# A written list of 2,418 step numbers in place of a list scheduler for the first phase of a decoder-layer kernel

## The chip, the cores and the metric

The kernel runs on one core of a Trainium2 chip. The metric is the device time of one execution, in microseconds (us); the median of the runs before the change is 1961.02 us.

## The reference

One decoder layer over 1024 tokens of width 1024, in float32. The input is normalised and multiplied by `w_in`. Eight query heads of width 64, in two key groups, then run three attentions whose results are added with learned gates: over compressed keys, over selected blocks (with 16 blocks of 64 keys and `n_sel` 16 every block is taken, so this one is causal attention over all keys), and over a window of 512. A second branch gates 512 channels with a triangular 128x128 product in chunks. Both are normalised and multiplied by `w_out`, and a mixture of 32 experts, four per token, follows.

```
h = rmsnorm(x, norm1_g);  z = h @ w_in
o_attn = nsa_attention(q, kc, vc, k_sel, vs, k_win, vw, gates)
o_gm = spatial_gating(zu, zv, gm_v_norm_g, gm_w_s, gm_b_s)
x = x + concat(rmsnorm(o_attn), rmsnorm(o_gm)) @ w_out
x = x + moe(rmsnorm(x, norm2_g), ...)    # top 4 of 32, clamped SwiGLU
```

## The kernel before

Every float32 product is made of three half-precision products: each operand is split into a high part (a copy on ACT) and a low part (the difference, on DVE), and PE multiplies high by high, high by low and low by high. Most stages therefore hand work round in a ring: PE into PSUM, ACT reads it (high), DVE reads it (low), PE again.

The program has two large phases. The **first phase** runs to the router. Its parts are: the transposes of x (line 418), 72 products of x with `w_in` (lines 468 to 470, nine pieces of columns by eight token tiles; `L438` and `L442` split the weights), the compressed keys, the gating branch (`L670`, `L679`, `L683`), the attention, the product with `w_out` (lines 1337 to 1339, one row tile at a time) and the choice of experts (`L1368` to `L1414`). The attention is cut into 48 units of one group, one query tile and one branch. A unit has scores (`L935`, `L936`, into one of three PSUM banks `s`), distances and row maximum in one DVE pass (`L939`), the exponential on ACT (`L919`), and then for each block of keys four transposes on PE (`L976`, into one of three banks `b`), the high part (`L980`, ACT), the low part (`L984`, DVE) and the product with the values (`L996`, PE). `L959` and `L960` make a unit's weights, `L1009` applies them, and POOL adds the three branches (`L1025`, `L1021`).

The **second phase** computes the experts. Its weights come in pieces of 1 MB through five buffers (`L1773`), are split (`L1780` on ACT, `L1783` on DVE) and multiplied (`L1826` to `L1828`).

The order of each engine's instructions is fixed when the program is built. Each stage is registered as steps: `op(engine, cost, function, due, reads, writes)`. `Plan.run` then keeps, for each engine, the time at which it is free, and takes as the next step the one that can start first; steps that can start within 0.05 us of each other are ordered by `due`. The emitted instructions run on the chip in that order on each engine, and wait for each other by semaphores; the planner's own times go nowhere else. In the first phase each `due` was shifted by a number of a table, `WHEN`, one for each group of steps (`plan.group()` opens the next group). A step that needs another engine's result was taken to get it 0.25 us after that one's end, or 2.25 us where it is a load of SP:

```
lag = lag if lag is not None else 2.25 if eng == "sp" else 0.25
```

The experts have a plan of their own, of the same class, without a table: `plan = Plan(rings)`. Rings such as `psS=(3, 1)` and `psT=(3, 1)` in the first plan are the banks `s` and `b`: a step that takes one waits until the user three turns earlier is done.

Of the kernel before, what the change touches and what calls it, by code (L numbers as in the profile page):

```python
# [21 lines left out]
D = 1024  # L22
# [14 lines left out]
def visits(room):  # L37
# [36 lines left out]
WHEN = [  # L74
# [60 lines left out]
class Plan:  # L135
# [8 lines left out]
    def group(self):  # L144

        self.at += 1
# [110 lines left out]
def layer_kernel(ctx: ExitStack, tc: tile.TileContext, x, norm1_g, w_in, q_norm_g, k_norm_g, cmp_pos,  # L257
# [873 lines left out]
    def biases(due):  # L1131
# [34 lines left out]
        for n in range(2):  # L1166
            op("pe", 0.95, lambda n=n: up(n), due, r=[r], w=[b[n]])
# [879 lines left out]
```

## Time and profile before

| what | value |
|---|---|
| median of 3 runs | 1961.02 us (1959.91 to 1964.04) |
| the profiled execution | 1960.88 us, of which the span of its instructions is 1959.1 us |
| PE busy | 1865.3 us, 95% of the span |
| DVE, ACT, POOL busy | 1653.5, 1468.2, 783.0 us |
| mean granted TensorE clock | 0.985 |

The span runs from the first to the last instruction; 1.8 us of the execution lie outside it. An engine's busy time counts the instructions, not the waits of its queue. PE's matmuls are pipelined and their ends are modelled, so that the next one can start before the row of the last one ends; how much work PE has is therefore better read from the distance between the starts of matmuls that follow each other without a wait. A granted clock of 1.00 is 2.4 GHz, 0.50 is 1.2 GHz.

### The profile page before, as it was taken

The numbers are of one execution on the slowest core, as the hardware profiler recorded it, in microseconds if no ns is written. First come the engines' busy times: TensorE is split into PE (matmuls) and PEld (weight loads), VectorE is DVE, ScalarE is ACT, GpSimd is POOL, SyncE is SP. The second block draws the span as 40 slices with busy tenths as digits, with TensorE's granted clock in tenths as the row PEclk, the third lists the DMA queues.
The fourth block names the chain that finished last, engine by engine and source line by source line (L and its number), as shares of the span: only waits on it lengthen the run. The fifth ranks groups of instructions, "written<-read, shape, count | busy, mean of one in ns | idle before, by whom it ended". The sixth has DMA issues, their size and how long they took to land.

```text
span 1959.1 us, 60049 instructions
## 1 busy us (share of the span) xinstructions
PE 1865.3 (95%) x25170; PEld 1708.0 (87%) x25170; DVE 1653.5 (84%) x2844; ACT 1468.2 (75%) x2310; POOL 783.0 (40%) x667
## 2 busy tenths in 40 slices
PE   7999999898996999999999999999999999999996
PEld 6898777666655898899999999999999999999995
DVE  5577887778777898798998999999999999999893
ACT  6566878757554675777877888788888888888883
POOL 0111112345551454344344443353444535455432
PEclk9999999999996999999999999999999999999998
DMA  4320102221125998899999999999999999999993
GB/s 162 84 60 12 45 12 65 87 71 45 66 76 191 299 342 275 282 328 322 336 332 331 339 350 356 338 354 358 363 352 352 350 359 355 351 356 365 361 348 90
DMA packets 244775, 485.88 MB, mean 248 GB/s; under 512 B 20034, under 2 KB 29394, under 8 KB 244498
## 3 DMA queue, kind: packets, MB, share of 16 engines
q1 hardware_dynamic: 230658, 441.19, 64.2%
q0 software_dynamic: 12800, 40.79, 9.2%
q8 instruction: 199, 3.26, 0.7%
q14 instruction: 78, 0.64, 0.1%
q10 hardware_dynamic: 1040, 0.00, 0.0%
HBM read 450.94 MB, written 31.00 MB: 246 GB/s over the span
## 4 chain that ended last, share of the span: by engine, by line
PE 75%; DVE 9%; DMA 7%; ACT 5%; issue 3%; POOL 1%; SPq 0%; DVEq 0%; POOLq 0%; ACTq 0%
PE g L1826 16%; PE g L1827 16%; PE g L1828 16%; PE s L468 3%; PE s L469 3%; PE s L470 3%; DVE par L939 3%; DMA xw<-in_w_gate_up_dram 2%; PE b L1894 2%; PE b L976 2%; PE o L996 2%; DVE wl L1783 2%; DMA raw<-in_w_gate_up_dram 2%; ACT wh L1780 2%; PE b L1752 1%
## 5 line engine op out<-in xcount | busy, mean ns | idle before, releaser
L1826 PE MATMUL g<-xar,wh 128*128 128x88 f16 (+21 forms) x4096 | 770.8, 229 | 0.5 <-ACT ott L1877 0.5
L1827 PE MATMUL g<-xar,wh 128*128 128x88 f16 (+21 forms) x4096 | 771.0, 229 | 0.0
L1828 PE MATMUL g<-xar,wl 128*128 128x88 f16 (+21 forms) x4096 | 770.5, 229 | 0.1
L1783 DVE SCALAR_TENSOR_TENSOR wl<-xw,wh 128x2048 f16<-128x2048 f32 x308 | 714.4, 2326 | 40.2 <-ACT wh L1780 34.6
L1780 ACT ACTIVATE wh<-xw 128x2048 f16<-128x2048 f32 x308 | 626.4, 2036 | 157.2 <-PE g L1827 86.9
L1827 PEld LDWEIGHTS <-wh 128*128 128x128 f16 x6144 | 600.4, 98 | 15.9 <-issue 4.8
L1826 PEld LDWEIGHTS <-wh 128*128 128x128 f16 x6144 | 600.8, 98 | 10.7
L1828 PEld LDWEIGHTS <-wl 128*128 128x128 f16 x6144 | 600.3, 98 | 11.0 <-DVE wl L1783 0.3
L1854 POOL TENSOR_TENSOR aar<-t,aar 128x136 f16<-128x136 f32 (+21 forms) x256 | 360.1, 1423 | 469.1 <-ACT aar L1852 441.9
L1826 PE MATMUL g<-aar,wh 128*128 128x120 f16 (+21 forms) x2048 | 385.4, 229 | 3.8 <-DVE t L1841 3.8
L1828 PE MATMUL g<-aar,wl 128*128 128x120 f16 (+21 forms) x2048 | 385.4, 229 | 0.0
L1827 PE MATMUL g<-aar,wh 128*128 128x120 f16 (+21 forms) x2048 | 385.4, 229 | 0.0
L1841 DVE TENSOR_SCALAR t<-g,bias 128x120 f32<-128x120 f32 (+20 forms) x512 | 170.8, 364 | 32.5 <-PE g L1828 22.4
L1780 ACT ACTIVATE wh<-raw 128x2048 f16<-128x2048 f32 x76 | 154.8, 2037 | 39.6 <-PE g L1827 21.5
L1904 POOL DMA_INDIRECT out_dram<-orow,ix x51 | 124.8, 2447 | 147.7 <-ACT orow L1897 84.4
L1783 DVE SCALAR_TENSOR_TENSOR wl<-raw,wh 128x2048 f16<-128x2048 f32 x76 | 175.4, 2308 | 8.3 <-ACT wh L1780 7.7
L1722 POOL DMA_INDIRECT xg<-xn_d,ix x51 | 128.0, 2510 | 117.2 <-PE g L1828 47.2
L468 PE MATMUL s<-wh,xw 128*128 128x256 f16 (+1 forms) x576 | 158.2, 275 | 1.2 <-DVE mx L939 1.1
L469 PE MATMUL s<-wl,xw 128*128 128x256 f16 (+1 forms) x576 | 158.1, 275 | 0.0
L470 PE MATMUL s<-wh,xw 128*128 128x256 f16 (+1 forms) x576 | 158.0, 274 | 0.0
L1025 POOL TENSOR_TENSOR ob<-ob 128x512 f32<-128x512 f32 x32 | 40.7, 1270 | 191.9 <-DVE ob L1009 164.9
L1849 DVE SCALAR_TENSOR_TENSOR t<-t 128x136 f32<-128x136 f32 (+21 forms) x256 | 100.4, 402 | 18.1 <-ACT t L1846 15.1
(380 smaller groups left out, 2942.0 us busy)
## 6 DMA issues: line engine op xcount, KB each, us to landing
xw<-in_w_gate_up_dram SPq DMA_DIRECT2D x205, 1024.0 KB
xw<-in_w_down_dram SPq DMA_DIRECT2D x103, 1024.0 KB
raw<-in_w_gate_up_dram SPq DMA_DIRECT2D x51, 1024.0 KB
raw<-in_w_down_dram SPq DMA_DIRECT2D x25, 1024.0 KB
wr<-in_w_in_dram SPq DMA_DIRECT2D x16, 512.0 KB
xs<-in_x_dram SPq DMA_DIRECT2D x8, 512.0 KB
wr<-in_w_out_dram SPq DMA_DIRECT2D x8, 512.0 KB
x<-in_x_dram SPq DMA_DIRECT2D x8, 512.0 KB
```

What stands on the lines that cost most here:

```text
L468: mm(o, xa, wh, start=(k == 0), stop=False)
L469: mm(o, xa, wl, start=False, stop=False)
L470: mm(o, xb, wh, start=False, stop=(k == KD - 1))
L1722: nc.gpsimd.indirect_dma_start(out=xg.t[:w], out_offset=None, in_=xn_d, in_offset=bass.IndirectOffsetOnAxis(ap=ix.t[:w, 0:1], axis=0))
L1780: nc.scalar.activation(ws.v[0], raw_.v, AF.Copy, scale=SW)
L1783: nc.vector.scalar_tensor_tensor(ws.v[1], raw_.v, SW, ws.v[0], op0=ALU.mult, op1=ALU.subtract)
L1826: mm(o, wh, xa, start=(kh == 0 and k == 0), stop=False)
L1827: mm(o, wh, xb, start=False, stop=False)
L1828: mm(o, wl, xa, start=False, stop=(kh == 1 and k == 3))
L1841: nc.vector.tensor_scalar(t.t[:, s, :c], ps[s].t[:, :c], self.bias(2 * h + s), m, op0=ALU.add, op1=o)
L1854: plan.op("pool", 0.9 + c / 440, lambda: nc.gpsimd.tensor_tensor(out=self.a[:, h, 1], in0=t.t[:, 1, :c], in1=self.a[:, h, 0], op=ALU.subtr ...
L1904: self.plan.op("pool", 2.0, lambda: nc.gpsimd.indirect_dma_start(out=out, out_offset=bass.IndirectOffsetOnAxis(ap=ix.t[:w, 0:1], axis=0), ...
```

## The change

The first phase's steps are emitted in the order of a list, `STEPS`: 2,418 numbers, one for each step in the order in which the code registers them. The scheduler's choice is left out where such a list is given. `WHEN`, `group()` and all its calls go. Some planned costs and all planned handover times get other numbers. Where a list is given they decide nothing; the experts' plan has no list, so for it the new default handovers (`HANDOVER`) count: 4.0 us behind a load of SP in place of 2.25, and 0.15 to 0.22 behind the engines in place of 0.25.

```
-WHEN = [
-    1346.1, 299.4, 788.3, -170.5, 1081.8, 114.3, -565.0, 519.3, -380.7, 1232.6, -82.9, 90.6, -610.6, 327.8, 529.5, -374.5, 361.1,
...
+STEPS = [
+    0, 7, 67, 4, 1, 8, 19, 9, 68, 31, 10, 69, 11, 5, 12, 43, 13, 16, 70, 14, 6, 79, 17, 2, 71, 189, 72, 15, 20, 76, 3, 73, 55, 74,
...
+HANDOVER = dict(sp=4.0, pe=0.22, act=0.17, dve=0.15, pool=0.2)
...
-    def op(self, eng, cost, fn, due, r=(), w=(), use=(), lag=None, table=None):
+    def op(self, eng, cost, fn, due, r=(), w=(), use=(), lag=None, table=None, own=0.0):
...
-        due += self.when[self.at] if self.at < len(self.when) else 0
...
-        lag = lag if lag is not None else 2.25 if eng == "sp" else 0.25
+        lag = HANDOVER.get(eng, 0.25) if lag is None else lag
...
-        for _ in range(n):
+        for turn in range(n):
             best = None
-            for eng, cand in avail.items():
+            for eng, cand in () if self.seq else avail.items():
...
+            if self.seq:
+                best = ready(self.seq[turn]), self.seq[turn]
...
-            end[i] = free[eng] = t + cost
+            end[i] = free[eng] = max(t, free[eng]) + cost
...
-                     m=(2, 0), ogt=(1, 0), x1=(2, 0), xn=(1, 0), xt=(1, 0), xp=(1, 0), s2=(2, 0), jo=(1, 1)), WHEN)
+                     m=(2, 0), ogt=(1, 0), x1=(2, 0), xn=(1, 0), xt=(1, 0), xp=(1, 0), s2=(2, 0), jo=(1, 1)), STEPS)
...
-        op("pe", 0.45, run, due, r=[("wsT", g)] + toks, w=[y])
+        op("pe", 0.86, run, due, r=[("wsT", g)] + toks, w=[y])
...
-        op("pe", 2.7, hidden, due + 8, r=[w1] + parts, w=[hp], use=[xc])
+        op("pe", 3.55, hidden, due + 8, r=[w1] + parts, w=[hp], use=[xc])
```

How the instructions move is seen at three places. The new file has other line numbers; its line in the rows below is told where the text needs it.

First, ACT in the attention, at the third of the four places where it makes the gating branch's GELU (`L683`, now 724; `L980` is now 1015, `L1126` 1158, `L679` 720, `L919` 956, `L846` 884). Before:

```order
L980 ACTIVATE ph<-b 128x512 x3
L679 ACTIVATE ubuf<-s 128x256
L683 ACT_TABLE_LOAD
L683 ACTIVATE ubuf<-ubuf 128x1024
L980 ACTIVATE ph<-b 128x512 x2
L1126 ACTIVATE xw<-wr,gms 128x1024
L980 ACTIVATE ph<-b 128x512 x2
L690 ACTIVATE ubuf,sso<-vb 128x256 x4
```

Now:

```order
L1158 ACTIVATE xw<-wr,gms 128x1024
L720 ACTIVATE ubuf<-s 128x256
L724 ACT_TABLE_LOAD
L724 ACTIVATE ubuf<-ubuf 128x1024
L1015 ACTIVATE ph<-b 64x512
L1158 ACTIVATE xw<-wr,gms 128x1024
L884 ACTIVATE q_160<-b,gqh 128x512
L956 ACT_TABLE_LOAD
L956 ACTIVATE par,su<-par,mx 128x896
L1015 ACTIVATE ph<-b 128x512
```

In the old order two high parts of transposed probabilities, then a piece of `w_out`, then two more follow the GELU; in the new one the high parts stand apart. PE's order has to do with it: before, 16 transposes (four blocks of keys) stand in a row there,

```order
L996 LDWEIGHTS ph
L996 MATMUL o<-vv,ph 128x128
L996 LDWEIGHTS pl
L996 MATMUL o<-vv,pl 128x128
L976 MATMUL b<-ident,par 128x128 x16
L996 LDWEIGHTS ph
L996 MATMUL o<-vv,ph 128x128
```

and at the last of these four blocks PE now has, with scores (972 and 973) and a product with the values (1031) around each block's four transposes (1011),

```order
L1031 MATMUL o<-vv,ph 128x128
L1031 LDWEIGHTS pl
L1031 MATMUL o<-vv,pl 128x128
L972 LDWEIGHTS q_160
L972 MATMUL s<-ka_149,q_160 128x256
L973 LDWEIGHTS q_160
L973 MATMUL s<-kb_150,q_160 128x256
L1011 MATMUL b<-ident,par 128x128 x4
L972 LDWEIGHTS q_159
L972 MATMUL s<-ka_149,q_159 128x256
L973 LDWEIGHTS q_159
L973 MATMUL s<-kb_150,q_159 128x256
```

In all of the first phase, transposes of probabilities stood in 81 runs of one block, 21 of two, 7 of three and 1 of four; now there are 98, 16, 6 and 0.

Second, DVE at the first of the router's choices (`L1368` to `L1414`, now 1394 to 1440). Before:

```order
L1009 TENSOR_TENSOR ob<-o,su 128x512
L1368 TENSOR_REDUCE lr<-b 128x32
L1369 SCALAR_TENSOR_TENSOR lg<-lr,brb 128x32
L1411 MAX mx_5614<-lg 128x8
L1412 COPY rep<-mx_5614 128x4
L1413 MATCH_REPLACE lr<-rep,lg 128x32
L1414 TENSOR_TENSOR sel_5618<-lg,lr 128x128
L959 RECIPROCAL su<-su 128x4
L960 TENSOR_TENSOR su<-su,gates 128x4
L984 SCALAR_TENSOR_TENSOR pl<-b,ph 128x512
L1257 SCALAR_TENSOR_TENSOR ml<-b,mh 128x512
```

Now (976 is `L939`, 994 to 996 are `L958` to `L960`):

```order
L1394 TENSOR_REDUCE lr<-b 128x32
L1395 SCALAR_TENSOR_TENSOR lg<-lr,brb 128x32
L1437 MAX mx_5458<-lg 128x8
L1438 COPY rep<-mx_5458 128x4
L1439 MATCH_REPLACE lr<-rep,lg 128x32
L1440 TENSOR_TENSOR sel_5462<-lg,lr 128x128
L976 ISA ptc,mx<-s,dcmp 128x64
L976 ISA mx 128x1
L976 ISA par,mx<-s,dist,mx 128x512
L976 ISA mx 128x1
L994 TENSOR_SCALAR su<-su 128x4
L995 RECIPROCAL su<-su 128x4
```

Before, a low part for PE (`L984`) stood three rows behind the choice; now row maxima and a unit's weights stand there.

Third, DVE at the opening of the second phase, where the list doesn't reach: `xar` and `ixf`, `ix`, `gtt` are the gathered tokens and their indices and gates, `oh` the one-hot rows that pick them (`L1701`). Before:

```order
L1783 SCALAR_TENSOR_TENSOR wl<-xw,wh 128x2048
L1757 COPY xar<-b 128x8x80
L1783 SCALAR_TENSOR_TENSOR wl<-xw,wh 128x2048
L1757 COPY xar<-b 128x8x80
L1701 TENSOR_TENSOR oh<-iot,slot_r 128x8x120
L1701 TENSOR_TENSOR oh<-iot,slot_r 128x8x112
L1718 TENSOR_REDUCE gtt<-b 80x1 x2
L1783 SCALAR_TENSOR_TENSOR wl<-xw,wh 128x2048
L1713 TENSOR_REDUCE ixf<-b 120x1
L1714 CAST ix<-ixf 120x1
```

Now (every line of it is 26 higher):

```order
L1809 SCALAR_TENSOR_TENSOR wl<-xw,wh 128x2048
L1783 COPY xar<-b 128x8x80
L1727 TENSOR_TENSOR oh<-iot,slot_r 128x8x120
L1727 TENSOR_TENSOR oh<-iot,slot_r 128x8x112
L1744 TENSOR_REDUCE gtt<-b 80x1 x2
L1809 SCALAR_TENSOR_TENSOR wl<-xw,wh 128x2048
L1739 TENSOR_REDUCE ixf<-b 120x1
L1740 CAST ix<-ixf 120x1
L1744 TENSOR_REDUCE gtt<-b 120x1
L1727 TENSOR_TENSOR oh<-iot,slot_r 128x8x112
L1727 TENSOR_TENSOR oh<-iot,slot_r 128x8x96
L1739 TENSOR_REDUCE ixf<-b 112x1
```

The second `wl` stood behind one copy; two one-hot rows and a pair of gates now stand ahead of it too. The third, row eight before, comes only behind this piece, so behind two more one-hot rows.

At the start of the program the second half of the first piece of `w_in` (line 433, SP) is now issued ahead of the third tile of x.

## Rows read from the trace of the kernel before

**Rows 1.** The page, part 1, the whole span
```profile
PE 1865.3 (95%) x25170; PEld 1708.0 (87%) x25170; DVE 1653.5 (84%) x2844; ACT 1468.2 (75%) x2310; POOL 783.0 (40%) x667
```

**Rows 2.** Windows: busy us (count) by engine, granted clock, DMA share, GB/s
```profile
9.20:175.00 165.80, 164.30 (x1473) 145.69 (x1474) 105.83 (x323) 100.58 (x266) 17.93 (x32) 1.00 0.27 76
175.00:352.40 177.40, 166.96 (x1616) 137.07 (x1614) 146.60 (x403) 145.82 (x338) 33.35 (x46) 1.00 0.13 40
352.40:597.50 245.10, 224.84 (x1937) 155.30 (x1935) 187.05 (x590) 152.88 (x378) 120.53 (x224) 0.97 0.21 69
690.00:1959.00 1269.00, 1238.42 (x19249) 1205.56 (x19246) 1136.38 (x1380) 1006.33 (x1257) 580.38 (x341) 0.99 0.99 333
```

**Rows 3.** PE's waits, 9 to 597.5 us: total us, times, longest
```profile
PE b L976 <- DVE pl L984: 9.0, 11, 1.7
PE o L996 <- DVE pl L984: 8.6, 7, 3.4
PE s L935 <- DVE mx L939: 4.6, 18, 0.7
```

**Rows 4.** Timeline of PE: start, us; starts that follow each other
```profile
120.56 0.27 PE L468 MATMUL s<-wh,xw 128*128 128x256 f16 x1
120.67 0.27 PE L469 MATMUL s<-wl,xw 128*128 128x256 f16 x1
444.58 0.22 PE L996 MATMUL o<-vv,pl 128*128 128x128 f16 x1
444.63 0.22 PE L996 MATMUL o<-vv,ph 128*128 128x128 f16 x1
```

**Rows 5.** Lines of PE, 9 to 596 us: busy, mean ns, idle before
```profile
L468 PE MATMUL s<-wh,xw 128*128 128x256 f16 (+1 forms) x576 | 158.2, 275 | 1.2 <-DVE mx L939 1.1
L996 PE MATMUL o<-vv,ph 128*128 128x128 f16 x528 | 70.8, 220 | 0.0
L976 PE MATMUL b<-ident,par 128*128 128x128 f32 x528 | 76.8, 279 | 12.7 <-DVE pl L984 9.0 <-DVE mx L939 2.9 <-ACT par L919 0.4
L1337 PE MATMUL s<-xw,mh 128*128 128x512 f16 x128 | 48.6, 380 | 0.6 <-DVE mx L939 0.6
```

**Rows 6.** Timeline of ACT, PE, DVE at 328 us
```profile
328.34 1.28 ACT L683 ACT_TABLE_LOAD   x1
331.96 0.66 PE L976 MATMUL b<-ident,par 128*128 128x128 f32 x4 [1.40 <-DVE pl L984]
331.21 1.29 DVE L984 SCALAR_TENSOR_TENSOR pl<-b,ph 128x512 f16<-128x512 f32 x2 [3.44 <-ACT ph L980]
```

**Rows 7.** Timeline of POOL, DVE, PE at 446 us
```profile
446.21 2.61 POOL L1025 TENSOR_TENSOR ob<-ob 128x512 f32<-128x512 f32 x2 [10.26 <-DVE ob L1009]
446.30 1.23 DVE L1369 SCALAR_TENSOR_TENSOR lg<-lr,brb 128x32 f32<-128x32 f32 x1
450.72 0.23 PE L996 MATMUL o<-vv,pl 128*128 128x128 f16 x1 [3.39 <-DVE pl L984]
```

**Rows 8.** Windows in which the granted clock is under 1
```profile
385.00:390.00 5.00, 5.00 (x25) 4.62 (x25) 1.33 (x3) 1.93 (x4) 1.26 (x1) 0.50 0.17 54
451.00:455.00 4.00, 3.61 (x28) 3.15 (x25) 3.76 (x21) 2.95 (x9) 1.86 (x10) 0.57 0.00 0
```

**Rows 9.** Source line L960: ns min/median/max of one
```profile
L960 DVE TENSOR_TENSOR su<-su,gates x48: 162/165/2186, 154.5 to 558.9; 128x4 f32<-128x4 f32 x48
```

**Rows 10.** Timeline at the start
```profile
2.16 0.69 SPq L395 DMA_DIRECT2D xs<-in_x_dram  x1
16.36 0.42 PE L468 MATMUL s<-wh,xw 128*128 128x256 f16 x1
```

**Rows 11.** Timeline of DVE at the start of the experts
```profile
626.60 2.29 DVE L1783 SCALAR_TENSOR_TENSOR wl<-xw,wh 128x2048 f16<-128x2048 f32 x1 [1.63 <-ACT wh L1780]
629.21 2.15 DVE L1701 TENSOR_TENSOR oh<-iot,slot_r 128x960 bf16<-128x960 f32 x2
```

**Rows 12.** Experts, 690 us to the end: DVE's costliest line
```profile
L1783 DVE SCALAR_TENSOR_TENSOR wl<-xw,wh 128x2048 f16<-128x2048 f32 x295 | 684.5, 2327 | 37.3 <-ACT wh L1780 33.0 <-PE g L1827 1.8 <-issue 1.1
```

More of the change, by code (lines that the diff above doesn't have):

```diff
@@ L135, with __init__ @@
 class Plan:
-    def __init__(self, rings, when=()):
+    def __init__(self, rings, seq=()):
         self.rings = {k: (n, dyn, []) for k, (n, dyn) in rings.items()}
         self.ops, self.last, self.readers, self.scope = [], {}, {}, ()
-        self.when, self.at = when, 0
-    def group(self):
-        self.at += 1
+        self.seq = seq
     def slot(self, ring):
@@ L188, in op @@
         deps.discard(i)
-        lag = lag if lag is not None else 2.25 if eng == "sp" else 0.25
-        self.ops.append((eng, cost, fn, due, deps, take, slots, after, lag, table))
+        lag = HANDOVER.get(eng, 0.25) if lag is None else lag
+        self.ops.append((eng, cost, fn, due, deps, take, slots, after, lag, table, own))
     def swap(self, fn, due, closes, opens):
@@ L212, in ready @@
         def ready(i):
-            eng, _, _, _, deps, take, _, after, _, _ = ops[i]
-            t = max([end[d] + (ops[d][8] if ops[d][0] != eng or ops[d][8] > 1 else 0.0) for d in deps], default=0.0)
+            eng, _, _, _, deps, take, _, after, _, _, _ = ops[i]
+            t = max([end[d] + (ops[d][8] if ops[d][0] != eng or ops[d][8] > 1 else ops[d][10]) for d in deps], default=0.0)
             for s in after:
@@ L235, in run @@
                         best = (t, i)
-            if best is None:
+            if self.seq:
+                best = ready(self.seq[turn]), self.seq[turn]
+            if best is None or best[0] is None or need[best[1]]:
                 raise RuntimeError(f"no order: {[(c[:5], [(ops[i][3], [s.ring for s in ops[i][5]]) for i in c[:5]]) for c in avail.values()]}")
             t, i = best
-            eng, cost, fn, _, _, take, slots, _, _, table = ops[i]
+            eng, cost, fn, _, _, take, slots, _, _, table, _ = ops[i]
             if table not in (None, loaded):
@@ L388, in x_tile @@
     def x_tile(a):
-        plan.group()
         due = 1.5 * a
@@ L402, in x_tile @@
         due = XT * a
-        plan.group()
         op("act", 1.18, stat, due + 3, r=[x_], w=[ss])
@@ L411, in x_half @@
     def x_half(a, h, x_, due):
-        plan.group()
         b, tk = plan.slot("psT"), ("x", a, h)
@@ L425, in piece_half @@
     def piece_half(i, kh):
-        plan.group()
         _, c0, n, _ = PIECES[i]
@@ L445, in piece_half @@
         op("sp", 1.5, load, due - (14 if i else 0), w=[r])
-        plan.group()
         op("act", 1.6, hi, due - (8 if i else -3), r=[r, "g1"], w=[ws])
@@ L453, in piece_tile @@
     def piece_tile(i, a, ws):
-        plan.group()
         kind, _, n, o0 = PIECES[i]
@@ L475, in take @@
     def take(kind, o0, a, ps, due):
-        plan.group()
         r, rs = 1.0 / (SW * SZ), ("rstd1", a)
@@ L524, in norms @@
     def norms(lo, n, toks, key, due):
-        plan.group()
         rms(lambda: rsq[:, :, lo:lo + n], lambda: ssq[:, :, lo:lo + n], DH, ("rsq", key), due, toks)
@@ L558, in q_norms @@
     def q_norms(o0, due):
-        plan.group()
         lo = o0 // DH
@@ L597, in gating @@
     def gating(d0, due, late):
-        plan.group()
         def mask():
@@ L612, in gelu @@
                 nc.scalar.activation(v, v, AF.Gelu_apprx_tanh)
-        plan.group()
         op("act", 3.8, gelu, due, r=["gmc"], w=toks, table="gelu")
@@ L622, in gating_end @@
     def gating_end(due):
-        plan.group()
         op("dve", 0.1, lambda: nc.vector.tensor_tensor(out=ssv[:, 1], in0=sso[:, 0], in1=sso[:, 1], op=ALU.add), due,
@@ L632, in spatial @@
     def spatial(g, due, wsr):
-        plan.group()
         b = plan.slot("psT")
@@ L642, in row_sums @@
     def row_sums(due, toks):
-        plan.group()
         junk = plan.slot("ubuf")
@@ L656, in normed @@
     def normed(a, due, toks):
-        plan.group()
         v = lambda: PO["vb"][:, a]
@@ L664, in gate @@
     def gate(g, due, toks):
-        plan.group()
         y = plan.slot("psT")
@@ L710, in compress @@
     def compress(s_, due):
-        plan.group()
         w1 = plan.slot("w1")
@@ L788, in compress_end @@
     def compress_end(due):
-        plan.group()
         def sums():
@@ L823, in stack_half @@
     def stack_half(src, r, due, gains, key, on_pool, toks, hf):
-        plan.group()
         d, a = plan.slot("dup"), slice(4 * hf, 4 * hf + 4)
@@ L898, in front @@
         def front(self, j):
-            plan.group()
             g, i, br, nk = self.g, self.i, self.br, self.nk
@@ L946, in score @@
             plan.op("dve", 0.14 + w / 1085, dist_max, T3 + US * due, r=[s, "dist"], w=[mx, ("p", self.p, j)],
-                    use=[self.p])
+                    use=[self.p], own=0.23)
         def weigh(self):
-            plan.group()
             g, i, br, su = self.g, self.i, self.br, self.su
@@ L965, in back @@
         def back(self, k):
-            plan.group()
             g, i, br, n, o = self.g, self.i, self.br, self.n, self.o
@@ L996, in pv @@
                         mm(o.t[:, j * P:(j + 1) * P], p.t[:n, j], va, start=st and j + m == 0, stop=en and j + m == 4)
-            plan.op("pe", 0.43, turn, due, r=[("p", self.p, j) for j in range(4)], w=[b], use=[self.p, o])
+            plan.op("pe", 0.44, turn, due, r=[("p", self.p, j) for j in range(4)], w=[b], use=[self.p, o])
             plan.op("act", 0.48, hi, due, r=[b], w=[ph])
@@ L1003, in weighted @@
         def weighted(self, due):
-            plan.group()
             ob, o, su = self.ob, self.o, self.su
@@ L1013, in finish @@
     def finish(g, i, units, due):
-        plan.group()
         due = T3 + US * due
@@ L1024, in finish @@
         for x in (b, c):
-            plan.op("pool", 1.56, lambda x=x: nc.gpsimd.tensor_tensor(out=a.t, in0=a.t, in1=x.t, op=ALU.add), due, r=[x], w=[a])
-        plan.op("pool", 0.9, last, due, r=[a] + [("st", (h,), hf) for h in range(4 * g, 4 * g + 4) for hf in range(2)], w=[("o", g, i)])
+            plan.op("pool", 1.35, lambda x=x: nc.gpsimd.tensor_tensor(out=a.t, in0=a.t, in1=x.t, op=ALU.add), due, r=[x], w=[a])
+        plan.op("pool", 0.7, last, due, r=[a] + [("st", (h,), hf) for h in range(4 * g, 4 * g + 4) for hf in range(2)], w=[("o", g, i)])
     def open_attention():
@@ L1115, in out_row @@
     def out_row(k, due):
-        plan.group()
         r, g, a = plan.slot("wr"), gms[:, k:k + 1], (k + 4) % 8
@@ L1131, in biases @@
     def biases(due):
-        plan.group()
         r, o, b = plan.slot("x1"), plan.slot("x1"), [plan.slot("psT") for _ in range(3)]
@@ L1166, in biases @@
         for n in range(2):
-            op("pe", 0.95, lambda n=n: up(n), due, r=[r], w=[b[n]])
-        op("pe", 0.95, down, due, r=[r], w=[b[2]])
+            op("pe", 1.75, lambda n=n: up(n), due, r=[r], w=[b[n]])
+        op("pe", 1.75, down, due, r=[r], w=[b[2]])
         for n in range(3):
-            op("act", 0.8, lambda n=n: take(n), due + 1, r=[b[n], "rt"], w=[o])
+            op("act", 0.51, lambda n=n: take(n), due + 1, r=[b[n], "rt"], w=[o])
         op("sp", 2.0, lambda: nc.sync.dma_start(bias_d.rearrange("e p c -> p e c"), o.t[:, :24 * NE].rearrange("p (e c) -> p e c", c=24)), due + 2,
@@ L1211, in mix @@
         def mix(self):
-            plan.group()
             a, due, end = self.a, self.due - 12, self.end
@@ L1242, in turn @@
         def turn(self, s, src, tok, due):
-            plan.group()
             b, m, tk = plan.slot("psT"), self.m, ("m", self.a, s)
@@ L1261, in proj @@
         def proj(self):
-            plan.group()
             zs = [plan.slot("psS") for _ in range(2)]
@@ L1343, in add @@
         def add(self, z, nh):
-            plan.group()
             x1, c = self.x1, slice(nh * 512, nh * 512 + 512)
@@ L1350, in route @@
         def route(self):
-            plan.group()
             due, a, q = self.due + (13 if self.end else 17), self.a, self.q
@@ L1490, in layer_kernel @@
     plan.scope = ("W0",)
-    op("pool", 2.5, rt_ramps, start(9) + 1, w=["rt"])
+    op("pool", 1.05, rt_ramps, start(9) + 1, w=["rt"])
     op("dve", 3.4, rt_consts, start(9) + 2, r=["rt"], w=["rt"])
@@ L1496, in layer_kernel @@
     plan.scope = ("W",)
-    op("pool", 1.0, lambda: nc.gpsimd.dma_start(PO["g2b"], bcast(norm2_g, D)), start(9), w=["g2b"], lag=3.25)
+    op("pool", 1.0, lambda: nc.gpsimd.dma_start(PO["g2b"], bcast(norm2_g, D)), start(9), w=["g2b"], lag=5.0)
     op("dve", 0.8, rows_consts, start(9) + 5, r=["g2b", "rt"], w=["g2b"])
```

153 rows, old and new, of tables (STEPS, WHEN) are left out of this document.

## The prediction

> **What bounds the kernel now.** I read the busy line first: PE is busy 1865.3 of 1959.1 us [rows 1], so PE sets the time and the change can win only what PE still loses. Then the windows, to see where it loses. From 690 us to the end, among the experts, PE is busy 1238.4 of 1269 us and the DMA queues at 0.99 [rows 2]; the new list does not reach that stretch. In the first phase PE shows 1.5 us of idle time up to 175 us, 10.4 from there to 352.4 and 20.3 from 352.4 to 597.5 [rows 2]. The gain of a better order can therefore come from some 31 us of shown waits behind 175 us, and from little else.
>
> Next, what those waits are. PE's list of waits names three rings: the transposes' banks `b` wait 11 times for DVE's low part, 9.0 us; the product with the values waits 7 times for the same line, 8.6 us, of which one is 3.4; the score banks `s` wait 18 times for DVE's row maximum, 4.6 us [rows 3]. By lines the transposes lose most, 12.7 us, the products with `w_in` 1.2 and those with `w_out` 0.6 [rows 5]. So DVE's answer comes too late, and in 36 places, not everywhere. Two of them show why. At 331.96 us PE waits 1.40 us in the run of four blocks of transposes: the fourth block needs the bank of the first, DVE's low part of that one has itself waited 3.44 us for ACT's high part, and ACT was at the GELU, with 1.28 us of table load ahead of it [rows 6]. At 450.72 PE waits 3.39 us: the router's first choice stands ahead of the low part on DVE, and one small row of it lasts 1.23 us while POOL adds branches for 2.61 [rows 7].
>
> Two smaller losses lie beside this. PE's clock is granted at 0.57 from 451 to 455 us, which is between 1.2 and 2.4 GHz and directly behind the wait of 3.39; and at 0.50, so 1.2 GHz throughout, from 385 to 390 [rows 8]. And a wait shows only where the modelled end of the last matmul has passed: a product with `w_in` lasts 0.27 us in the rows while the next starts 0.11 behind it [rows 4], so a stop can hide up to 0.16 us.
>
> **The change, part by part.** No instruction's work changes: the same steps of the first phase stand in another order. What an order can win is the spare between the moment a stage hands a result out and the moment the program lets PE need it. I counted that for every stage of the rings in both orders, with PE's own work in between taken at the starts' distances [rows 4, 6] (a product with `w_in` 0.11 us, one with the values 0.056, four transposes 0.5), less the path through ACT and DVE. It is an estimate from the order and those durations, and shows where PE is exposed, not how long it waits.
>
> - Transposes: places with under 2 us of spare for a bank's turn go from 19 to 11, by 42%; runs of three or four blocks from 8 to 6.
> - Score banks with under 0.5 us: 106 to 63, by 41%. The gain comes from products with `w_in`, which now stand among the attention instead of in longer pieces.
> - Products with the values with under 1 us: 74 to 54, by 27%.
>
> Weighted by the waits of rows 3, that is 9.0 x 0.42 + 8.6 x 0.27 + 4.6 x 0.41 = 8.0 of 22.2 us, or 36%. Spread over all 30.7 us shown behind 175 us [rows 2], the first term is **-11 us**. Its bounds are 0 (the waits only move) and -30.7.
>
> The wait at 450.72 goes or shrinks in this: in the new order row maxima and a unit's weights stand behind the choice on DVE, and the low part comes later, so that what is late next is a row maximum, with three score banks to cover it. With the wait I let the dip at 451 go: 4 us at 0.57 lose 4 x 0.43 = **-1.7 us**. The dip at 385 has no long wait directly ahead of it in the rows that I can tie to a step, so I leave it; if it went as well, 5 x 0.5 = 2.5 us more.
>
> Hidden stops: 19 + 106 + 74 = 199 exposed places become 128. The 71 that go could hide 0.16 us each, so between 0 and 11 us; most places with little spare don't stop at all (36 waits are shown), so I take about a third, **-4 us**.
>
> The start: the second half of the first weights is issued ahead of the third tile of x. PE's first product now starts at 16.36 us, behind loads issued from 2.16 on [rows 10]; fewer transposes stand ahead of it. The rest of that stretch is loaded at 0.27 of the DMA's capacity and PE idles only 1.5 us [rows 2], so what it wins is **-0.5 us**, between 0 and -1.5.
>
> The new costs of the products (0.45 to 0.86 and so on) decide nothing where a list is given. The new handovers do change something, in the experts' plan: DVE's order differs at 62 places there, ACT's at 74, PE's at 12. The largest is the opening. The second low part of weights (2.29 us at 626.60) used to stand ahead of two one-hot rows (2.15 us) [rows 11], and now stands behind them, the third behind two more. The second one waits 1.63 us for ACT before it starts, so that much of the first pair is covered; the rest, 2.15 - 1.63 = 0.5, and up to 2.15 for the second pair are not, if PE needs those weights at once. I take **+1 us**, between 0 and +2.7. Without the cover it would be 4.3. The other places I cost at nothing: PE has a whole piece of weights in hand while DVE makes the next, and DVE's waits there are for ACT and PE (37.3 us in all [rows 12]), so its order has room. That is the cover; rival four takes it away.
>
> POOL is what the count leaves out. A unit's weights (`L960`, 128x4) take 165 ns in the median but up to 2186 [rows 9], and the choice's row 1.23 us beside POOL's add [rows 7]: such rows of DVE are held while POOL is at work on SBUF, and which ones are held is a matter of when the two meet. The new order shifts all of these meetings. The Trainium skill ("SBUF — State Buffer", section "Who interferes with whom") says that a DVE instruction with two inputs in SBUF and a GpSimd instruction that reads SBUF lock each other out for the whole instruction. The 2186 ns agree with it. By the rows alone the meetings cost as much as before, on average, and the sum stands; by the rule an order planned with fixed durations pays for each that it newly puts on the path, and the sum would come out near zero, as rival three.
>
> Sum: 11 + 1.7 + 4 + 0.5 - 1 = 16.2 us less. The profiled execution is 1960.88 us, 0.14 under the median of the runs, 1961.02; so **1945 us**.
>
> **The rivals.** *Two: nearly all waits go.* If DVE's low parts are never late again, the 30.7 us shown, both dips (4.2) and the start's half go: 1960.9 - 35.4 = 1926. For it speaks that only 36 places wait at all and that their longest two have causes an order can remove. Against it, 128 of 199 exposed places remain, and DVE is busy 187 of 245 us from 352.4 on [rows 2], so that shifts of its work run into other work.
>
> *Three: the waits move.* POOL's adds last 1.3 us each [rows 7], and a DVE row that meets one is held about as long. If ten to twelve low parts or row maxima are newly behind such a row, 13 to 16 us come back and the time is 1958 to 1961. For it: the wait at 450.72 is one. Against it: the old order meets POOL just as blindly.
>
> *Four, slower: the experts' order costs.* There DVE is busy 1136 of 1269 us [rows 2], the low part of weights is 2.33 us long [rows 12], and PE waits for it. If one of these stands behind rows that it stood ahead of, PE stops. At 0.26 us for each of the 62 places the gain of 16 is gone; at 0.35 it is +22 - 16, so 1967 us. For it: the handover behind a load rises from 2.25 to 4.0, and in a stretch with the DMA at 0.99 a load's place is what counts. Against it: SP's order moves at four places only, PE's at 12, and PE idles 30.6 us of 1269 now, which is room that most of such shifts use up before they cost.
>
> **How the numbers follow.** A difference under 0.2%, 4 us, can hardly be told from no change. The forecast, 1932 to 1956, gets 0.56; rival two 0.17, rival three (1957 to 1965) 0.13, rival four 0.14. Faster is the first two, 0.73; the same 0.13; slower 0.14. For eight in ten the range leaves out the lower half of rival two and most of rival four: 1928 to 1963.
>
> **What would show it.** The last product with `w_out` should end near 582 us in place of 597.5, and from there to the end the trace should stay within 3 us of 1361.6. PE's waits for `L984`, 17.6 us over the two rings, should fall to about 11, without one of 3 us; the clock should be 1.00 about the first choice. A first phase that ends where it did, with the same waits under other names, would be rival three; an end that comes early but is given back behind 690 us, with PE's idle time there well over 30.6, rival four. The forecast is wrong in its first term if the exposed places that I counted are not the ones that wait.

## The result, and the profile after

The changed kernel takes 1936.77 us (median of 4 runs, 1935.22 to 1937.02), the kernel before in the same comparison 1962.53; the ratio is 0.9856, with a 95% interval from 0.9837 to 0.9875. The forecast of 1945 us had the direction and too little of the size: of its profiled execution's 1960.88 us the kernel lost 23.9, to 1937.02, where the sum said 16.2.

The page's first part of the changed kernel, which answers to [rows 1]:

```profile
PE 1859.3 (96%) x25170; PEld 1709.5 (88%) x25170; DVE 1645.7 (85%) x2844; ACT 1465.0 (76%) x2309; POOL 786.3 (41%) x667
```

Every count is the same but ACT's, which has one table load less. Next the last product with `w_out` (1339 before, 1367 now): min/median/max in ns, first and last start in us. The first row is of before, the second of the change.

```profile
L1339 PE MATMUL s<-xw,ml x128: 377/379/380, 394.6 to 595.4; 128*128 128x512 f16 x128
```

```profile
L1367 PE MATMUL s<-xw,ml x128: 378/379/380, 388.9 to 571.7; 128*128 128x512 f16 x128
```

It starts at 571.7 in place of 595.4, 23.7 us earlier. From there to the end of the span are 1935.2 - 571.7 = 1363.5 us, and were 1959.1 - 595.4 = 1363.7. (The prediction took 597.5, the end of its window, for this product; the comparison is made with its own start.) So in this pair of traces all of the gain lies in the first phase, and the experts' new order costs and brings nothing that they show. How closely is a matter of the spread: with one order of the experts, this last stretch took 1362.6 us in one profile and 1368.5 in another (e5 and e4 below). The windows of the change, as in [rows 2]:

```profile
9.20:175.00 165.80, 163.25 (x1457) 145.05 (x1458) 100.56 (x308) 98.20 (x264) 17.12 (x31) 1.00 0.29 82
175.00:352.40 177.40, 169.32 (x1663) 140.26 (x1661) 149.82 (x419) 152.52 (x345) 35.89 (x47) 0.99 0.14 43
352.40:571.70 219.30, 211.84 (x1887) 148.24 (x1887) 181.10 (x587) 145.50 (x369) 117.66 (x222) 0.98 0.21 68
690.00:1936.00 1246.00, 1217.08 (x18916) 1184.87 (x18916) 1115.77 (x1355) 987.79 (x1235) 574.53 (x336) 0.99 0.99 334
```

Behind 175 us PE shows 8.1 + 7.5 = 15.5 us of idle time, where it showed 30.7. PE's waits up to 580 us (total us, times, longest), against [rows 3]:

```profile
PE s L972 <- DVE mx L976: 5.8, 8, 2.0
PE b L1011 <- DVE pl L1019: 4.9, 5, 2.4
PE b L1011 <- DVE mx L976: 1.8, 4, 0.6
PE o L1031 <- DVE pl L1019: 1.1, 3, 0.6
```

The low parts cost 6.0 us in place of 17.6, the row maxima at the score banks 5.8 in place of 4.6.

What lies under the modelled ends can be had from the starts. I took each of PE's rows up to the last product with `w_out`, let it last as long as rows of its line and shape usually take to the next start, and called the rest lost. The work is 523.2 us before and 522.7 now; lost are 63.2 and 39.8, so 37% less. Stops of over 0.3 us were 54 and are 26, those from 0.1 to 0.3 were 102 and are 65. Of the time lost, the granted clock, in windows of 5 us, took up to 6.9 us before and takes up to 5.2 now (a stretch at 0.50 is counted with half its length, and costs less where PE would have waited anyway).

### The profile page after: what moved, and what is told of

Read it like the earlier page. It is cut to its first block, busy times and chain, and to the rows that moved or that the text cites. A ratio compares the mean times of both kernels' runs of the same rounds, so it can differ in the third digit from the quotient of the medians.

```text
span 1935.2 us, 60032 instructions
## 1 busy us (share of the span) xinstructions
PE 1859.3 (96%) x25170; PEld 1709.5 (88%) x25170; DVE 1645.7 (85%) x2844; ACT 1465.0 (76%) x2309; POOL 786.3 (41%) x667
## 4 chain that ended last, share of the span: by engine, by line
PE 82%; DVE 7%; DMA 6%; ACT 3%; issue 2%; POOL 0%; POOLq 0%; SPq 0%; DVEq 0%; ACTq 0%
PE g L1852 18%; PE g L1853 18%; PE g L1854 18%; DMA xw<-in_w_gate_up_dram 4%; PE s L519 3%; PE s L520 3%; PE s L521 3%; PE o L1031 3%; PE b L1011 3%; PE b L1920 2%; DVE wl L1809 2%; ACT wh L1806 2%; PE b L1778 1%; PE s L1365 1%; PE s L1366 1%
## 5 line engine op out<-in xcount | busy, mean ns | idle before, releaser
L1880 POOL TENSOR_TENSOR aar<-t,aar 128x136 f16<-128x136 f32 (+21 forms) x256 | 382.4, 1519 | 469.9 <-ACT aar L1878 446.4
L1930 POOL DMA_INDIRECT out_dram<-orow,ix x51 | 116.6, 2286 | 138.6 <-ACT orow L1923 92.1
L1748 POOL DMA_INDIRECT xg<-xn_d,ix x51 | 116.3, 2281 | 121.7 <-PE g L1854 39.6
L956 ACT ACTIVATE par<-par,mx 128x640 f32<-128x640 f32 (+7 forms) x128 | 93.2, 730 | 23.0 <-DVE mx L976 22.2
```

The lines of the kernel that those rows point to most:

```text
L1748: nc.gpsimd.indirect_dma_start(out=xg.t[:w], out_offset=None, in_=xn_d, in_offset=bass.IndirectOffsetOnAxis(ap=ix.t[:w, 0:1], axis=0))
L1880: plan.op("pool", 0.9 + c / 440, lambda: nc.gpsimd.tensor_tensor(out=self.a[:, h, 1], in0=t.t[:, 1, :c], in1=self.a[:, h, 0], op=ALU.subtr ...
L1930: self.plan.op("pool", 2.0, lambda: nc.gpsimd.indirect_dma_start(out=out, out_offset=bass.IndirectOffsetOnAxis(ap=ix.t[:w, 0:1], axis=0), ...
```

## Experiments

The start of the last product with `w_out` is the finest measure here. The same list gave 571.7 and 571.9 us in two profiles, another 561.9 and 562.1 on two chips. The old order varies more: in e6 it is 2.3 us later at the first product with `w_out`, though nothing ahead of that was moved. So differences of 2 us from the one profile of before say little. Unless another kernel is named, an edit is made to the changed kernel.

**e1: the experts as before.**

```
-HANDOVER = dict(sp=4.0, pe=0.22, act=0.17, dve=0.15, pool=0.2)
+HANDOVER = dict(sp=2.25, pe=0.25, act=0.25, dve=0.25, pool=0.25)
```

> The new list for the first phase, and the old handovers (2.25 us behind a load, 0.25 behind an engine) for the experts' plan, so that the experts' instructions stand as before the change. If all of the gain lies in the first phase, as the two traces say (1363.7 and 1363.5 us from the last product with w_out to the end), the time is that of the change, 1936.8, within 2 us; by the predicted +1 us for the experts' opening it would be 1936. If the new handovers had brought part of the gain, 1940 or more; if they had cost what the gain in the first phase hides, 1933 or less.

Ratio to before 0.9866 (0.9847 to 0.9885), median 1939.49. Its last product, as above:

```profile
L1367 PE MATMUL s<-xw,ml x128: 378/379/379, 389.2 to 571.9; 128*128 128x512 f16 x128
```

The median is above the 1936.8 named, but so is before's in this comparison (1965.96); e2 and e3, with the new handovers and the same comparison, have 1937.79 and 1938.86. Less their last products, 1367.6, 1368.7 and 1367.5 us remain of these medians for e1, e2 and e3. No difference is seen between the two orders of the experts; but the runs of one kernel lie 2.4 us (e1), 3.8 (e2) and 8.0 (e3) apart, so one of a microsecond or two could not be seen.

**e2: a held row is moved.** In the trace of the change the longest stop at a score bank has this cause. Its rows of POOL, DVE and PE (start and length in us; in brackets the wait and what ended it):

```profile
252.74 2.35 POOL L725 TENSOR_TENSOR vb<-vb,ubuf 128x1024 f32<-128x1024 f32 x1 [14.14 <-ACT ubuf L724]
253.15 1.98 DVE L580 TENSOR_SCALAR rsq<-ssq 128x32 f32<-128x32 f32 x1
255.87 0.58 PE L972 MATMUL s<-ka,q 128*128 128x512 f16 x1 [2.00 <-DVE mx L976]
```

The row of 32 columns ends at 255.13, just behind POOL's product (255.09). The edit, a cut of `STEPS` (503 is the guess, 504 the POOL step behind it):

```
-    552, 503, 1041, 982, 1049, 1042, 984, 945, 974, 983, 1050, 1036, 504, 946, 997, 553, 985, 947,
+    552, 1041, 982, 1049, 1042, 984, 945, 974, 983, 1050, 1036, 946, 997, 553, 985, 503, 504, 947,
```

> In the new list one step of DVE (the first guess of q's norms, L580 to L582) and the POOL step behind it stand 15 steps later, so that this row of 128x32 no longer meets POOL's product of 2.35 us at 252.7. In the trace of the change that row lasts 1.98 us, PE waits 2.00 us for the row maximum behind it, and the clock is 0.66 in the five us after. If the hold by POOL is the cause and the wait goes for good: 2.0 + 1.7 = 3.7 us less, 1933. If another row of DVE is held in its place, or the next wait takes it up: 1937, within 1 us.

Ratio 0.9863 (0.9844 to 0.9882), which can't be told from the change's. The trace can. The moved row and PE's stops behind it, the last product, and the window from 255 us:

```profile
256.14 0.17 DVE L579 TENSOR_SCALAR rsq<-ssq 128x32 f32<-128x32 f32 x1
...
257.40 0.38 PE L971 MATMUL s<-ka,q 128*128 128x512 f16 x1 [0.85 <-DVE mx L975]
261.49 0.63 PE L879 MATMUL b<-ident,dup 128*128 128x128 f32 x4 [0.70 <-DVE dup L866]
```

```profile
L1366 PE MATMUL s<-xw,ml x128: 377/379/379, 386.4 to 569.1; 128*128 128x512 f16 x128
```

```profile
255.00:260.00 5.00, 4.03 (x34) 2.74 (x33) 4.29 (x17) 4.67 (x15) 2.46 (x11) 1.00 0.00 0
```

The row takes 0.17 us, so POOL had held it for 1.8. The wait of 2.00 is gone, and so is the dip of the clock at 255, which is this window of the change:

```profile
255.00:260.00 5.00, 4.13 (x21) 2.20 (x21) 4.49 (x15) 3.98 (x12) 2.98 (x13) 0.66 0.00 0
```

How much of the 3.7 us lasts is seen at the last product with `w_in`, 85 us on: it starts at 341.8 in the change, at 340.4 here, and at 341.1 in e3, where this row is not moved.

```profile
L521 PE MATMUL s<-wh,xw x576: 271/273/283, 13.8 to 341.8; 128*128 128x256 f16 x171, 128*128 128x280 f16 x21
L520 PE MATMUL s<-wh,xw x576: 271/273/417, 13.9 to 340.4; 128*128 128x256 f16 x171, 128*128 128x280 f16 x21
L520 PE MATMUL s<-wh,xw x576: 271/273/283, 13.7 to 341.1; 128*128 128x256 f16 x171, 128*128 128x280 f16 x21
```

So 1.4 us last; stops such as the 0.85 and 0.70 take the rest. And e3 is 0.7 us ahead with its clock at 1.00 from 255 on, although PE's wait there is the same 2.00:

```profile
255.97 0.38 PE L971 MATMUL s<-ka,q 128*128 128x512 f16 x1 [2.00 <-DVE mx L975]
255.00:260.00 5.00, 3.58 (x25) 2.10 (x25) 4.86 (x17) 3.96 (x13) 3.10 (x13) 1.00 0.01 2
```

The dip can therefore not be put down to this wait alone, and half of the 1.4 us came in e3 without the edit. The 2.6 us at the last product hold 1.2 more, which came up at the low part of 361.42: PE waits 1.23 us for it here, where it waited 2.43 in the change.

```profile
360.80 0.66 PE L1010 MATMUL b<-ident,par 128*128 128x128 f32 x4 [1.23 <-DVE pl L1018]
```

The hold was the cause of the wait; what its removal brought in its own stretch is 0.7 to 1.4 us, not 3.7.

The Trainium skill ("SBUF — State Buffer", section "Who interferes with whom") says that a tensor_scalar, though it has one SBUF operand, can enter a 2-port mode and then take the port pair that DVE shares with GpSimd, and that the loser blocks for the whole instruction. This row agrees as far as it goes: it ends 0.04 us behind POOL's. Which mode it ran in, no row shows.

**e3: the router's constants behind the low part.** What PE waited 2.43 us for in the change, rows of DVE and PE:

```profile
361.42 0.80 DVE L1019 SCALAR_TENSOR_TENSOR pl<-b,ph 128x512 f16<-128x512 f32 x1
362.26 1.11 PE L1011 MATMUL b<-ident,par 128*128 128x128 f32 x4 [2.43 <-DVE pl L1019]
```

The edit, a cut of `STEPS` (626 is the constants' step):

```
-    1367, 1540, 595, 1379, 626, 1357, 1478, 1534, 1511, 1389, 1368, 1358, 1505, 1537, 635, 1172, 1178, 636, 1351, 1479,
+    1367, 1540, 595, 1379, 1357, 1478, 1534, 1511, 1389, 1368, 1358, 1505, 1537, 635, 1172, 1178, 636, 1351, 626, 1479,
```

> In the new list the step of DVE that makes the router's constants (15 rows, 3.1 us from 358.3) stands behind the low part that it stood ahead of. In the trace of the change PE waits 2.43 us at 362.26 for that low part, and the clock is 0.66 from 360 to 365. If a long DVE step ahead of a low part is itself the cost: 2.4 + 1.7 = 4.1 us less, 1932.7. If DVE has no room there, the row maximum that came next is 3.1 us later, its exponential had waited 1.66 us for it already, and the wait moves: 1936 to 1938.

Ratio 0.9868 (0.9843 to 0.9894), the last product at 571.4. Now the row maximum comes late:

```profile
361.35 0.79 DVE L975 CUSTOM_DVE_ANT_0 par<-s,dist 128x512 f32<-128x512 f32 x1
362.20 0.38 PE L971 MATMUL s<-ka,q 128*128 128x512 f16 x1 [2.60 <-DVE mx L975]
```

A wait of 2.43 has become one of 2.60, and of the 0.7 us that this run was ahead 0.3 are left at the end. DVE has 3.1 us of other work there and PE needs both rows behind it; which stands first brought nothing.

**e6: the kernel before, the router's first choice moved.** The old order as a list, with the old handovers and one step (1210) moved:

```
-    1661, 1824, 1914, 1917, 1210, 1680, 1829, 1843, 1922, 1742, 1457, 1681, 1815, 1458, 1844,
+    1661, 1824, 1914, 1917, 1680, 1829, 1843, 1922, 1742, 1457, 1681, 1815, 1210, 1458, 1844,
```

> The kernel before in all but one step: the router's first choice (L1368 to L1414) stands behind the low part for which PE waited 3.39 us, and not two rows ahead of it. As the prediction had it, the wait and the dip of the clock at 451 go: 3.4 + 1.7 = 5.1 us less than before, 1957.4 against 1962.5. If the wait only moves (the choice now delays the low parts behind it, at 452.2 and 453.4, and the bank that it reads): 1961 to 1963.

Ratio to before 0.9999 (0.9986 to 1.0012). The products with `w_out`:

```profile
L1366 PE MATMUL s<-xw,ml x128: 377/379/379, 396.9 to 598.2; 128*128 128x512 f16 x128
```

From the first to the last are 201.3 us, where 200.8 were. (The first, ahead of the moved step, is 2.3 us later than in before; by the choice it is 3.0.) PE's stops there, in place of the 3.39 of [rows 7]:

```profile
451.24 0.63 PE L1010 MATMUL b<-ident,par 128*128 128x128 f32 x4 [2.05 <-DVE lr L1393]
453.94 0.66 PE L1010 MATMUL b<-ident,par 128*128 128x128 f32 x4 [1.18 <-DVE ml L1285]
455.60 0.66 PE L1010 MATMUL b<-ident,par 128*128 128x128 f32 x4 [1.00 <-DVE pl L1018]
```

```profile
455.00:460.00 5.00, 4.40 (x37) 4.32 (x38) 4.21 (x14) 2.93 (x9) 3.58 (x19) 0.66 0.00 0
```

The choice reads a bank `b`, so it now holds up the transposes; 3.39 us became 2.05 + 1.18 + 1.00 = 4.23, and the dip of the clock stands behind these stops, at 455 in place of 451 (3.0 us of that are the later start). The rival in the expectation was right, and with it falls a reason of the prediction (below).

**e7, e8: POOL's adds made small.** In the kernel before and in the change the sum of the branches is left out but for one column (the rest of the line is cut here):

```
-... nc.gpsimd.tensor_tensor(out=a.t, in0=a.t, in1=x.t, op=ALU.add) ...
+... nc.gpsimd.tensor_tensor(out=a.t[:, :, :1], in0=a.t[:, :, :1], in1=x.t[:, :, :1], op=ALU.add) ...
```

> The kernel before with POOL's 32 adds of branches (L1025, 1.27 us each) over 1 column in place of 128 per head, so that this sum is left out and nothing on DVE is held by it. In the trace of before 14.5 us of DVE's rows are longer than usual, some 7 us of it beside these adds. If the holds cost PE what they cost DVE: the last product with w_out starts 5 to 9 us earlier than 595.4. If most of them fall where nobody waits: 0 to 3 us earlier.

> The change with the same adds over 1 column (the sum of branches is left out). If the change gained by meeting POOL less, the two orders come closer without the adds: less than 20 us between the last products with w_out, where there are 23.7 now. If the gain has nothing to do with POOL: 22 to 26 us between them, and 571.7 falls by 0 to 3 us.

The last product of each, before first:

```profile
L1339 PE MATMUL s<-xw,ml x128: 377/379/379, 395.8 to 593.8; 128*128 128x512 f16 x128
```

```profile
L1367 PE MATMUL s<-xw,ml x128: 377/379/380, 384.2 to 565.5; 128*128 128x512 f16 x128
```

The old order wins 1.6 us by it and the new one 6.2; the distance grows from 23.7 to 28.3. Neither expectation of e8 held, and the change did not gain by meeting POOL's adds less. That it pays more for them than the old order does is not shown: these are one profile each, and the clock has a part in them. By its stretches at half clock up to the last product, e7 (first two rows) loses up to 8.6 us where before loses 6.9, and e8 (last two) 3.4 where the change loses 5.2.

```profile
356.00:360.00 4.00, 4.00 (x35) 3.93 (x33) 1.80 (x5) 2.74 (x8) 1.20 (x1) 0.57 0.48 174
379.00:394.00 15.00, 13.61 (x72) 12.35 (x72) 7.33 (x26) 6.42 (x18) 3.69 (x6) 0.54 0.32 85
353.00:357.00 4.00, 3.79 (x23) 2.61 (x24) 3.62 (x21) 4.00 (x14) 3.01 (x22) 0.57 0.60 168
373.00:378.00 5.00, 5.00 (x36) 4.66 (x36) 2.58 (x14) 2.78 (x8) 1.15 (x3) 0.66 0.53 130
```

That is up to 3.5 of the 4.6 us by which the two gains differ.

**e9, e10: every high part answered later.** In the kernel before and in the change:

```
 nc.scalar.activation(ph.t[:n], four(b)[:n], AF.Copy, scale=SP)
+nc.scalar.activation(ph.t[:n, 0, :64], four(b)[:n, 0, :64], AF.Copy, scale=SP)
```

> The kernel before with a second ACT row of 64 columns behind each of the 148 high parts of the probabilities (the same values again), so that each answer to PE is 0.2 to 0.3 us later and ACT has some 37 us more to do, of 223 where it is busy 153. If exposed places are what costs: each of the 18 waits for a low part is 0.25 us longer and as many new ones appear: 5 to 10 us, so the last product with w_out starts at 600 to 605.

> The change with the same second row. If its gain is more spare between handing out and needing back, it loses less than before does by the same delay: 2 to 6 us, last product with w_out at 574 to 578. If its list is good because it fits the durations that it was planned with, it loses more than before does: over 8 us, 580 or later, and the distance between the two shrinks under 20 us.

The added row (busy us, mean ns) in before and in the change:

```profile
L981 ACT ACTIVATE ph<-b 128x64 f16<-128x64 f32 (+1 forms) x148 | 32.9, 223 | 4.7
```

```profile
L1016 ACT ACTIVATE ph<-b 128x64 f16<-128x64 f32 (+1 forms) x148 | 33.1, 224 | 4.7
```

And the last product with `w_out`:

```profile
L1340 PE MATMUL s<-xw,ml x128: 377/379/379, 404.8 to 609.4; 128*128 128x512 f16 x128
```

```profile
L1368 PE MATMUL s<-xw,ml x128: 377/379/379, 392.8 to 582.7; 128*128 128x512 f16 x128
```

Before loses 14.0 us and the change 11.0, two to three times what I had expected. So a delay costs at many more places than the shown waits name, or ACT's 33 us of added work hold up its other rows; the two are not told apart. Neither theory of e10 held whole: the change loses over 8 us, but less than before does, and the distance grows, to 26.7.

The parts differ: up to the first of these products before loses 10.2 and the change 3.9; behind it 3.8 and 7.1. But half of before's loss in the first part can be the clock's. Its stretches at half clock there, in e9 and (last row) in before itself:

```profile
204.00:208.00 4.00, 4.00 (x35) 3.62 (x34) 3.05 (x10) 3.94 (x11) 0.00 (x0) 0.57 0.32 112
276.00:280.00 4.00, 4.00 (x35) 3.93 (x33) 2.41 (x6) 3.44 (x8) 0.00 (x0) 0.57 0.00 0
388.00:403.00 15.00, 13.61 (x71) 12.42 (x71) 7.24 (x26) 6.21 (x17) 4.75 (x5) 0.54 0.33 85
383.00:394.00 11.00, 9.62 (x48) 8.29 (x47) 5.37 (x20) 6.91 (x19) 1.36 (x2) 0.53 0.60 107
```

They cost up to 10.3 us in e9 and 5.2 in before; e10 and the change have the same there, about 5.2. Less the clock, 5.1 is left for before and 3.9 for the change, of one profile each. Whether the delay made the further dips is open. So more spare in the new order is suggested for the first part and not shown, and behind it the new order loses more.

**e11: the figures without the list.** The list is what the old scheduler makes of the new figures and the old `WHEN`.

> The change's durations and handovers, but its list replaced by what the old scheduler makes of them with the old table WHEN. If the better figures bring the gain: last product with w_out at 575 or earlier, as in the change. If the list brings it, and WHEN only fits the old figures: later than before's 595.4, by its own plan some 50 us.

```profile
L1366 PE MATMUL s<-xw,ml x128: 377/379/634, 389.4 to 648.8; 128*128 128x512 f16 x128
```

53.4 us later than before, 2010.59 us in all (one run). Better figures alone, with the table as it was, don't bring the gain. That the table fits only the figures that it was found with is the likely reason; a new table was not tried.

**e4, e5, e12: two further lists.** Both were made from the change's by moving or exchanging single steps where the planned end came earlier, or, now and then, a little later. Their first steps:

```
-    0, 7, 67, 4, 1, 8, 19, 9, 68, 31, 10, 69, 11, 5, 12, 43, 13, 16, 70, 14,    # the change
+    7, 8, 67, 68, 4, 9, 69, 1, 0, 10, 11, 70, 12, 71, 13, 5, 2, 72, 16, 6,      # e4
+    7, 67, 4, 8, 0, 1, 9, 19, 68, 10, 11, 5, 12, 31, 13, 16, 69, 70, 43, 6,     # e5, e12
```

> A third list for the first phase, all else as in the change. It was made from the change's list by moving single steps as long as the planned end came earlier, with the change's own durations and handovers and nothing else; its plan is 9 us shorter than that of the change. If durations and handovers are all that counts, the first phase ends some 9 us earlier than in the change (571.7 us at the start of the last product with w_out), at 563, and the time is 1928 where the change has 1937. If holds by POOL, which this plan doesn't know, and shifts among DVE's rows decide what is left: no gain, 570 or later, as it was when single waits were taken away (571.4 with the constants moved).

> A list made in the same way and from the same start, but with one rule more: DVE's rows with two operands in SBUF (a unit's weights, the norms' first guess, the splits of weights, the router's choice) and POOL's wide rows don't run at the same time. Its plan without that rule is as long as that of the list before. If holds by POOL are a large part of the 39.8 us that PE still loses in the change's first phase: at least 8 us earlier than the list without the rule, 555 to 562, so 1921 to 1928. If holds cost little in sum (9.6 us of longer DVE rows in the change's trace, most of them not waited for): within 3 us of the list without the rule.

> The list that keeps POOL's wide rows and DVE's rows with two operands apart, once more and timed in more rounds. If what its profile showed holds (last product with w_out 9.8 us ahead of the change's): ratio to before 0.9856 - 9.8 / 1962 = 0.981, and the last product at 561.9 within 0.5. If the list meets POOL otherwise from run to run: a later end and a ratio above 0.984.

The last product in e4 and in e12:

```profile
L1366 PE MATMUL s<-xw,ml x128: 377/379/389, 379.1 to 565.5; 128*128 128x512 f16 x128
```

```profile
L1366 PE MATMUL s<-xw,ml x128: 377/379/379, 379.5 to 562.1; 128*128 128x512 f16 x128
```

e4 gains 6.2 us on the change's first phase, of the 9 that its plan gave, e5 9.8 and e12 9.6. Medians and ratios: e4 1931.75, 0.9817 (0.9781 to 0.9853); e5 1928.48, 0.9824 (0.9802 to 0.9847); e12 1925.41 beside 1963.99 of before, 0.9801 (0.9783 to 0.9819). The interval of e12 lies below the change's, so this list beats both kernels. With the rule on POOL the list ends 3.6 us earlier than e4's: less than the 8 of the one theory, a little more than the 3 of the other. It is one list of each kind, and no run shows how far two searches without the rule lie apart, so the 3.6 us can't be given to the rule. DVE's rows of the first phase that last over 0.05 us longer than the median of their kind, nearly all beside a row of POOL, do so by 16.5 us in e4, 11.5 in e5 and 10.4 in the change: with the rule the list has fewer holds than without, but no fewer than the change. PE's waits in e5, of which the longest of the attention is 1.2 us:

```profile
PE o L1030 <- DVE pl L1018: 1.5, 2, 1.2
PE s L971 <- DVE mx L975: 1.4, 4, 0.6
PE b L1010 <- DVE pl L1018: 1.2, 3, 0.7
```

## Why the prediction came out as it did

It was right on the side and in what bounds the kernel: the gain came out of PE's stops in the first phase, where 37% of its lost time went. Term by term, us:

| term | predicted | measured |
|---|---|---|
| shown waits behind 175 us | -11 | -15.2 (30.7 to 15.5) |
| granted clock | -1.7 | -1.7 (6.9 to 5.2) |
| start, lost time up to 175 us | -0.5 | -0.6 (7.0 to 6.4) |
| hidden stops | -4 | -5.9 (what the rows above leave of 63.2 - 39.8) |
| experts | +1 | -0.2 in this pair, which can't show so little |

- **The first term was mis-sized**, 11 for 15.2; together with the hidden stops it makes 6 of the 7.7 us that the forecast was short. The prediction applied its 36% to the 30.7 us of shown waits, which fell by 49%, and took a third of a bound for the rest. On all 63.2 us of lost time the 36% would give 22.8, and the 63.2 could have been counted from the starts beforehand; but that all lost time fell by 37% is chance, since what is no shown wait behind 175 us fell by 25%. Nor do "only 36 places" wait: these are three rings of a longer list, and by the starts 156 stops last over 0.1 us.
- **The weights by ring were wrong**, and their mean too low: 36%, where the three rings together fell by 47%, from 22.2 to 11.8. Predicted: 42% off the transposes' waits for low parts, 27% off those of products with the values, 41% off the score banks'. Measured: 9.0 to 4.9 (46%), 8.6 to 1.1 (87%), 4.6 to 5.8 (more). A count of exposed places in an order does not say which of them stop.
- **The wait at 450.72 went, but not for the reason given.** The prediction said that the place of the choice makes it and that the clock's dip goes with it. In e6 one moved step gave nothing: the stop and the dip went to other rows. e3 shows the same for its wait. That the clock's term came out at 1.7 is therefore luck of the sum: the dip at 451 went, the one at 385 became shorter (0.66 from 378 to 383 now), and others came, 0.66 at 255 and at 360. The prediction also took the dip at 385 at half its size: it lasts from 383 to 394 (0.53, the last row of e9's windows) and costs up to 5.2 us, not 2.5.
- **The start** was right to about 0.1 us. **The experts'** +1 is neither confirmed nor refuted, since e1 to e3 can't see a microsecond.
- **One sign was worked out wrongly.** The terms of the first phase make 11 + 1.7 + 4 + 0.5 = 17.2, so its end belongs at 580.3 by the sum, not near 582.
- **Rival two** (nearly all waits go, 1926) did not come about with this list; e12, with another, ends there, at 1925. The room was there, and further search from the change's list took more of it, without the rule on POOL (e4) and with it.
- **Rival three** (holds by POOL eat the gain) did not come about. Its mechanism is shown at one place, a DVE row held for 1.8 us with a wait of PE behind it, worth 0.7 to 1.4 us (e2). That the new list as a whole pays more for POOL than the old one is not shown, since the clock can have most of the difference between e7 and e8.
- **Rival four** (the experts' order costs 16 to 22 us) is refuted by the result and by e1; a cost of a microsecond or two is not.

What carries the gain is thus no single place. Taking one late row away gave 2.6 us, nothing and nothing; new orders as a whole gave 23.7 and up to 9.8 more. That the order of the first phase makes the gain, and that it comes as fewer stops of PE, is shown by the starts, e1 and e11. That the spare between handing out and needing back is what makes the stops fewer is argued; e9 and e10 don't show it. Also open is why the clock falls where it does. Of some 28 us still lost in e5, its two stretches at half clock, at 355 to 362 and 368 to 372 us, are 5.1 at most.

## What to carry to other kernels

Where an engine that is busy four fifths of the time answers the one that bounds the kernel, a late row can't be judged alone: ask what stands behind it and needs the same time. Here two of three such edits only renamed the wait, and the third kept less than half of it in its own stretch. Size such a gain on all time lost between the starts of the bounding engine's instructions, not on the waits that a profile shows. If an order is planned, plan it as a whole; and a duration that was measured alone is not the one that a row has beside another engine (0.17 and 1.98 us here). Before a difference between two profiles is given to an edit, look at what the granted clock did in each.

## What the runs showed of the hardware

- A DVE row with one operand in SBUF (`L580`, 128x32) was held by POOL from 0.17 to 1.98 us (e2). POOL is held as well: its add at 354.04 in the change takes 2.17 us, beside a DVE row of 1.28 that began at 353.81, and 1.27 elsewhere.

```profile
348.80 1.27 POOL L1058 TENSOR_TENSOR ob<-ob 128x512 f32<-128x512 f32 x1
...
354.04 2.17 POOL L1058 TENSOR_TENSOR ob<-ob 128x512 f32<-128x512 f32 x1 [3.96 <-DVE ob L1043]
```

- PE's wait of 2.00 us at 255 was followed by a granted clock of 0.66 from 255 to 260 us in the change and of 1.00 in e3, with the same instructions up to there (rows with e2). A dip is not a fixed price of a wait.
- The end of the first phase repeats within 0.3 us for one new list (571.7 and 571.9; 561.9 and 562.1), while the rest of the program took 1362.6 us in e5's profile and 1368.5 in e4's, with the experts' instructions in one order. Two new lists are told apart by that row far better than by the total.
